# Attention of a two-layer decoder step: rotated rows gathered over two heads' tiles, the sink as a column of the scores, and the stage's instructions in a written order

## The chip, the cores and the metric

The kernel runs on one core of a Trainium2 chip. Its time is device microseconds of one launch; the table below gives the median of three runs and the one profiled execution. All inputs and outputs are float32 in device memory.

## The reference

One inference step of a decoder with two layers, for a prompt of 512 tokens and for 8 samples of one token each (position 2048, with a cached window of 127 + 1 keys). Width 1024, 16 heads of 64, 4 key/value heads, window 128, feed-forward width 2816. Layer 1 mixes tokens by pooling, layer 2 by attention; each layer is feed-forward, mixer, feed-forward. What the change touches is layer 2's attention:

```python
q = _rope((h @ w_q[j]).reshape(B, T, N_KV_HEADS, GROUP, HEAD_DIM), pos)   # rotates dims 0..15 of each 64
s = einsum('bnqkgd,bnskd->bnkgqs', q, k) * (HEAD_DIM ** -0.5)
s = where(mask, s, -inf)                    # d = qpos - kpos: 0 <= d < 128
m = maximum(max(s, -1), sink)               # one sink for each head
p = exp(s - m)
denom = sum(p, -1) + exp(sink - m)
o = einsum('bnkgqs,bnskd->bnqkgd', p / denom, v)
x = x + o @ w_o[j]
```

`_rope` replaces dims 0..7 by x1 cos - x2 sin and dims 8..15 by x2 cos + x1 sin and leaves dims 16..63.

## The kernel before

**Layout.** Activations stand transposed: eight tiles `x[k]` of 128 features by 520 tokens (512 of the prompt, 8 samples). A float32 matrix product is made of three matmuls on a high and a low part of each operand (`terms`, `mm`, L417); `split` (L241) makes the parts, the high one by ScalarE (L245), the low one by VectorE (L246).

**Weights.** The class `Weights` loads chunks of 1 MB on SyncE's queue into three `raw` buffers and splits them piece by piece on ScalarE (`wh`, L194) and VectorE (`wl`, L195), five pieces ahead of their use; `prefetch` is called where a piece is taken. A load is pinned behind what was written before it on SyncE; it waits for its buffer at the head of that queue.

**The order.** The instructions are given in the order of the program to a planner, which may move them by their due times, except those wrapped in `later`: such an instruction is pinned behind the one written just before it on its engine. In the attention stage of before, few are.

**The attention stage** (L1033 to L1341). Eight q tiles of 128 features, t = 0..7, each two heads e = 0, 1 of 64 rows. `q_part(t, h)` makes half of the product (24 matmuls), `q_evac(t)` copies it out of PSUM (L919), rotates it (L920 to L923: multiply by cos, shuffle the rows by 8 within groups of 32, multiply by sin, add, all on 128 rows), splits it, and copies the samples' columns to `qz` (L1063). A `Unit(t, h)` is two blocks of 128 queries of both heads of a tile; there are 16. `scores` (L1086 to L1088) makes 12 matmuls on 64 rows each and 256 keys, of which block 0 needs only 128. `softmax` adds the mask and takes the maximum (L1101, four times), brings it and the sinks together (L1115 to L1117), takes the exponentials with their sums (L1121) and that of the sink (L1129), adds and inverts (L1130, L1131) and scales the four parts (L1134 on ScalarE, L1136 on VectorE). `turn` transposes the scaled parts (L1146) and splits them (`xh`, `xl`). `values` multiplies by v (L1169) and copies to `oT` (L1181). The loop over n = 0..18 calls scores(n), q parts, turn(n-2), jobs, softmax(n), values(n-3) and the evacuations; jobs are the samples' own attention (L1219 to L1265) and the first half of the output product (`o_part(m, 0)`, L1278), of which the second half, `o_part(m, 4)`, follows the loop. PSUM has four pairs of banks (`duo`).

Of the kernel before, what the change touches and what calls it, by code (L numbers as in the profile page):

```python
# [45 lines left out]
C_END = C_AB + 2  # L46
# [7 lines left out]
def shape_constants():  # L54
# [11 lines left out]
    for h in (0, 64):  # L66
        c[h : h + 8, C_COS : C_COS + TOK] = cos
        c[h + 8 : h + 16, C_COS : C_COS + TOK] = cos
        c[h : h + 8, C_SIN : C_SIN + TOK] = -sin
        c[h + 8 : h + 16, C_SIN : C_SIN + TOK] = sin  # L70
    for gi, w in enumerate(WINS):
        for b in range(NS):
            for r in range(15 - (w - 1), 15):
                c[b * 15 + r, C_SEL + gi * NS + b] = 1.0
# [138 lines left out]
def yoco_step(ctx, tc, ins, outs):  # L213
# [26 lines left out]

    def split(dst, src, scale=None):  # L241

        hi, lo = dst
        if scale is None:
            S.activation(hi, src, AF.Copy)  # L245
            V.tensor_tensor(lo, src, hi.bitcast(F32), op=ALU.subtract)  # L246
        else:
            S.activation(hi, src, AF.Copy, scale=scale)
            V.scalar_tensor_tensor(lo, src, scale, hi.bitcast(F32), op0=ALU.mult, op1=ALU.subtract)

    def later(ins):

        return tc.keep_in_program_order(ins)
# [121 lines left out]
    def rstd_tok(t0=0, t1=5):  # L375
# [3 lines left out]
        for t in range(t0, t1):  # L379
            lo = t * P if t < 4 else 400  # L380
            T.matmul(pss[:, t : t + 1], acc[:, lo : lo + P], ones[:, 0:1], start=True, stop=True)  # L381
        v, y, t_ = (cp.tile([P, 5], F32, tag=n, name=n)[:, t0:t1] for n in ("nv", "ny", "nt"))
        later(V.tensor_scalar(v, pss[:, t0:t1], 1.0 / D, EPS, op0=ALU.mult, op1=ALU.add))
        V.tensor_scalar(y.bitcast(I32), v.bitcast(I32), 1, None, op0=ALU.arith_shift_right)
        V.tensor_scalar(y.bitcast(I32), y.bitcast(I32), -1.0, float(0x5F3759DF), op0=ALU.mult, op1=ALU.add)
        for it in range(3):
            V.tensor_tensor(t_, y, y, op=ALU.mult)
            V.scalar_tensor_tensor(t_, t_, -0.5, v, op0=ALU.mult, op1=ALU.mult)
            o = r_tok[:, t0:t1] if it == 2 else y
            V.scalar_tensor_tensor(o, t_, 1.5, y, op0=ALU.add, op1=ALU.mult)  # L390

    def rstd_samples():

        pr2 = pss_[0][:, 0, 8 : 8 + NS]
        T.matmul(pr2, r_tok[:, 4:5].broadcast_to([P, P]), ident[:, 112:120], start=True, stop=True)
        S.copy(R[:, SP:], pr2)
# [16 lines left out]
    def mm(w, kk, mov, banks, first, last, halves=(0, 1), pin=lambda ins: ins):  # L413
# [494 lines left out]
    kT = [kvp.tile([P, TOK], F32, tag="kT", name=f"kT{g}", bufs=2) for g in range(2)]  # L908
# [124 lines left out]
    with tc.tile_pool(name="at", bufs=2) as at:  # L1033
        cst = at.tile([P, 512], F32, name="cst", bufs=1)
        nc.scalar.dma_start(cst, consts[:, C_MASK : C_MASK + 512])
        csq = rawp.tile([P, 2, TOK], F32, tag="raw", name="csq")
        nc.scalar.dma_start(csq.rearrange("p a t -> p (a t)"), consts[:, C_COS : C_COS + 2 * TOK])
# [6 lines left out]

        r8 = at.tile([P, NB], F32, name="r8", bufs=1)
        nr8 = at.tile([P, NB, 2], F32, name="nr8", bufs=1)
        oS = at.tile([P, KT, NS], F32, name="oS", bufs=1)
        oT = [big.tile([P, SP], F32, tag="th", name="oT") for t in range(KT)]
# [6 lines left out]

        def q_evac(t, banks):
            qT = at.tile([P, TOK], F32, tag="qT", name="qT", bufs=1)
            rope(qT, banks, cosq, sinq, at, ("rp0", "rp1"))
            qq = pair(XX, [P, SP])
            split(qq, qT[:, :SP])  # L1060
            for e in range(2):
                rows = slice(e * 64, e * 64 + 64)
                V.tensor_copy(qz[t // 4][rows, e, t % 4, :], qT[rows, SP:])  # L1063
            return qq

        class Unit:
# [6 lines left out]
            def scores(self):  # L1073
# [5 lines left out]
                for bi, b in enumerate(self.bs):  # L1079
                    for e in range(2):  # L1080
                        rows = slice(e * 64, e * 64 + 64)
                        o = self.pe[e][:, bi * 256 : (bi + 1) * 256]
                        qc = slice(b * P, (b + 1) * P)
                        k0 = max(b - 1, 0) * P
                        kc_ = slice(k0, k0 + 256)
                        T.matmul(o, qh[rows, qc], kh[rows, kc_], start=True, stop=False)  # L1086
                        T.matmul(o, ql[rows, qc], kh[rows, kc_], start=False, stop=False)
                        T.matmul(o, qh[rows, qc], kl[rows, kc_], start=False, stop=True)  # L1088

            def softmax(self):  # L1090
                c0 = self.t * 8 + self.h * 4
                mx, nm, es, den = (at.tile([P, 4], F32, tag=n, name=n) for n in ("mx", "nm", "es", "den"))
                self.sms = []
                for bi, b in enumerate(self.bs):
                    if (2 * self.t + self.h) % 3 < 2:
                        sm = at.tile([P, 512], F32, tag="sm", name="sm", bufs=4)
                    else:
                        sm = kvp.tile([P, TOK], F32, tag="kT", name="sm", bufs=2)
                    mk = C_MASK if b == 0 else C_MASK + 256
                    for e in range(2):  # L1100
                        ins = V.tensor_tensor_reduce(  # L1101
                            out=sm[:, e * 256 : (e + 1) * 256],
                            in0=self.pe[e][:, bi * 256 : (bi + 1) * 256],
                            in1=cst[:, mk : mk + 256],
                            op0=ALU.add,
                            op1=ALU.max,
                            scale=1.0,
                            scalar=NEG,
                            accum_out=mx[:, bi * 2 + e : bi * 2 + e + 1],
                        )  # L1110
                        if self.t == 0:
                            later(ins)
                    self.sms.append(sm)
                nr = nr8[:, self.bs[0] : self.bs[1] + 1, :].rearrange("p b e -> p (b e)")
                later(V.tensor_tensor(nm, mx, nr, op=ALU.mult))  # L1115
                later(V.tensor_tensor(nm, nm, nsinks[:, c0 : c0 + 4], op=ALU.min))
                V.tensor_tensor(es, sinks[:, c0 : c0 + 4], nm, op=ALU.add)  # L1117
                part = lambda i: self.sms[i // 2][:, (i % 2) * 256 : (i % 2) * 256 + 256]
                for i in range(4):
                    b = self.bs[i // 2]  # L1120
                    S.activation(  # L1121
                        part(i),
                        part(i),
                        AF.Exp,
                        scale=r8[:, b : b + 1],
                        bias=nm[:, i : i + 1],
                        accum_out=den[:, i : i + 1],
                    )
                S.activation(es, es, AF.Exp)  # L1129
                V.tensor_tensor(den, den, es, op=ALU.add)  # L1130
                V.reciprocal(den, den)  # L1131
                for i in range(4):
                    if i % 2:
                        S.activation(part(i), part(i), AF.Copy, scale=den[:, i : i + 1])  # L1134
                    else:
                        V.tensor_scalar(part(i), part(i), den[:, i : i + 1], None, op0=ALU.mult)  # L1136

            def turn(self):
                self.pts = []
                both = duo()  # L1140
                for bi, b in enumerate(self.bs):
                    kts = (0,) if b == 0 else (0, 1)
                    pt = both[:, bi, :]
                    for kt in kts:
                        for e in range(2):
                            T.transpose(  # L1146
                                pt[:, kt * 256 + e * P : kt * 256 + (e + 1) * P],
# [305 lines left out]
```

## Time and profile before

| | us |
|---|---|
| median of 3 runs | 1697.96 |
| lowest, highest | 1693.47, 1698.41 |
| the profiled execution | 1691.85 |
| its span, first to last instruction | 1690.0 |
| TensorE busy | 1657.5 |
| VectorE busy | 1254.4 |
| ScalarE busy | 903.5 |

The profile's rows name an instruction by the line of the kernel, the engine, the operation and its tiles as out<-in, with partitions x elements. PE is TensorE's matmuls, PEld its weight loads, DVE VectorE, ACT ScalarE, POOL GpSimd, SP SyncE; a q behind an engine's name is its queue. Busy time is the union of the instructions' times; the duration of one includes a start that overlaps the end of the one before. The granted clock is TensorE's, 1.00 being full speed. In the waits stand the total, the number and the longest, in us. Of transfers the rows give KB each and the median time from issue to landing.

### The profile page before, as it was taken

What the parts mean: (1) busy time and instruction counts of PE and PEld (TensorE: products, weight loads), DVE (VectorE), ACT (ScalarE), POOL (GpSimd) and SP (SyncE); (2) the same over time, 40 slices, a digit from 0 to 9 for tenths busy, and PEclk for the clock granted to TensorE, in tenths of its full rate; (3) what the DMA queues carried; (4) which work ended last, traced back from release to release, by engine and by line L of the source; (5) the groups of instructions that cost most, each with busy time, mean ns of one, the idle gap of its engine ahead of it and who ended that gap; (6) DMA issues with size and microseconds to landing.
All of it is one profiled execution on the core that took longest, in us unless ns stands there. A gap on an engine that the chain in (4) does not pass through costs nothing.

```text
span 1690.0 us, 34449 instructions
## 1 busy us (share of the span) xinstructions
PE 1657.5 (98%) x13754; PEld 1642.7 (97%) x13754; DVE 1254.4 (74%) x2452; ACT 903.5 (53%) x1793; POOL 142.3 (8%) x176
## 2 busy tenths in 40 slices
PE   9999999999999999999999999999989999999997
PEld 8999999999999999999999999998879999999996
DVE  6866866887875875888775875888876885785776
ACT  6743643665652652656552652655886653463454
POOL 0101101000101101100101101100000100110100
PEclk9999999999999999999999999999899999999998
DMA  8546745652545855634745845642122554674631
GB/s 214 137 128 142 181 134 136 174 167 80 129 140 129 178 147 130 153 117 129 162 137 125 187 137 127 152 138 71 50 51 76 131 137 131 148 173 132 148 109 52
DMA packets 313327, 224.71 MB, mean 133 GB/s; under 512 B 9152, under 2 KB 289320, under 8 KB 313126
## 3 DMA queue, kind: packets, MB, share of 16 engines
q1 hardware_dynamic: 286416, 176.13, 36.8%
q0 software_dynamic: 22432, 40.26, 14.5%
q10 hardware_dynamic: 4318, 6.12, 1.2%
q8 instruction: 108, 1.77, 0.4%
q14 instruction: 53, 0.43, 0.1%
HBM read 180.11 MB, written 5.04 MB: 110 GB/s over the span
## 4 chain that ended last, share of the span: by engine, by line
PE 90%; DVE 4%; ACT 3%; DMA 1%; issue 1%; DVEq 0%; ACTq 0%
PE ps L443 45%; PE ps L417 41%; ACT sm L1121 1%; PE ps L1169 1%; PE ps L814 1%; DVE wl L195 1%; DMA pr<-in_bands_dram 1%; PE ps L839 1%; DVE sm L1101 1%; DVE xl L246 0%; ACT wh L194 0%; PE ps L1146 0%; PE ps L381 0%; PE ps L698 0%; DMA pr<-in_pool_w_dram 0%
## 5 line engine op out<-in xcount | busy, mean ns | idle before, releaser
L194 ACT ACTIVATE wh<-raw 128x512 fp32r<-128x512 f32 (+1 forms) x736 | 446.3, 621 | 544.8 <-PE ps L417 329.5
L195 DVE TENSOR_TENSOR wl<-raw,wh 128x512 fp32r<-128x512 f32 (+1 forms) x736 | 486.9, 676 | 200.7 <-ACT wh L194 197.2
L443 PE MATMUL ps<-th,wh 128*128 128x260 f32 x1216 | 343.7, 283 | 0.0
L443 PE MATMUL ps<-tl,wh 128*128 128x260 f32 x1216 | 343.1, 282 | 0.0
L443 PE MATMUL ps<-th,wl 128*128 128x260 f32 x1216 | 341.5, 282 | 0.0
L417 PE MATMUL ps<-hh,wh 128*128 128x260 f32 x1376 | 284.3, 285 | 2.3 <-DVE mx L1101 1.0
L417 PE MATMUL ps<-hl,wh 128*128 128x260 f32 x1376 | 283.2, 283 | 0.0
L417 PE MATMUL ps<-hh,wl 128*128 128x260 f32 x1376 | 280.7, 282 | 0.0
L443 PEld LDWEIGHTS ps<-tl,wh 128*128 128x128 f32 x1216 | 229.0, 188 | 0.0
L443 PEld LDWEIGHTS ps<-th,wh 128*128 128x128 f32 x1216 | 228.7, 188 | 0.2 <-ACT sa L523 0.2
L443 PEld LDWEIGHTS ps<-th,wl 128*128 128x128 f32 x1216 | 228.1, 188 | 0.0
L417 PEld LDWEIGHTS ps<-hh,wh 128*128 128x128 f32 x1376 | 213.5, 189 | 4.0 <-DVE mx L1101 1.2
L417 PEld LDWEIGHTS ps<-hl,wh 128*128 128x128 f32 x1376 | 215.2, 189 | 0.1
L417 PEld LDWEIGHTS ps<-hh,wl 128*128 128x128 f32 x1376 | 214.0, 189 | 0.0
L443 PE MATMUL ps<-xh,wh 128*128 128x260 f32 x672 | 188.3, 283 | 0.0
L443 PE MATMUL ps<-xl,wh 128*128 128x260 f32 x672 | 188.2, 283 | 0.0
L443 PE MATMUL ps<-xh,wl 128*128 128x260 f32 x672 | 184.2, 282 | 0.0
L159 POOL DMA_DIRECT2D raw<-raw x76 | 65.5, 862 | 1302.8 <-DMA raw<-in_ffn_w_up_dram 438.9
L417 PE MATMUL ps<-xh,wh 128*128 128x260 f32 x736 | 149.4, 285 | 0.6 <-ACT wh L194 0.6
L417 PE MATMUL ps<-xl,wh 128*128 128x260 f32 x736 | 149.5, 284 | 0.5 <-DVE xl L717 0.5
L417 PE MATMUL ps<-xh,wl 128*128 128x260 f32 x736 | 147.8, 283 | 0.1
L591 DVE TENSOR_TENSOR u<-ps,R 128x520 f32<-128x520 f32 (+1 forms) x99 | 67.2, 681 | 106.3 <-PE ps L417 106.3
(260 smaller groups left out, 2849.1 us busy)
## 6 DMA issues: line engine op xcount, KB each, us to landing
raw<-in_ffn_w_gate_dram SPq DMA_DIRECT2D x87, 512.0 KB, 3.9
raw<-in_ffn_w_up_dram SPq DMA_DIRECT2D x87, 512.0 KB, 5.4
raw<-in_ffn_w_down_dram SPq DMA_DIRECT2D x32, 1024.0 KB, 5.3
raw<-raw POOLq DMA_DIRECT2D x76, 256.0 KB, 3.3
S<-in_ffn_w_up_dram SPq DMA_DIRECT2D x76, 256.0 KB, 5.6
S<-raw POOLq DMA_DIRECT2D x76, 256.0 KB, 4.7
raw<-in_ffn_w_down_dram SPq DMA_DIRECT2D x16, 768.0 KB, 4.9
raw<-in_w_q_dram SPq DMA_DIRECT2D x8, 512.0 KB, 4.0
```

Of the source, the lines that this page charges most:

```text
L159: G.dma_start(blk(raw, 2, 1), blk(raw, 1, 1), accum_op=ALU.add)
L194: self.pin(nc.scalar.activation(dh, src, AF.Copy))
L195: self.pin(nc.vector.tensor_tensor(dl, src, dh.bitcast(F32), op=ALU.subtract))
L417: ins = T.matmul(banks[:, hf, :H], a[:, kk, :], hcols(b, hf), start=(first and i == 0), stop=(last and i == 2),)
L443: T.matmul(bank[:, :H], a[:, kk, :], b, start=(not more and kk == 0 and i == 0), stop=(kk == 3 and i == 2), skip_group_check=more,)
L591: V.tensor_tensor(parts(u), bank[:, hfs[0] : hfs[-1] + 1, :H], parts(R[:, c]), op=ALU.mult)
L814: T.matmul(o, a[:, s], b[:, kk, :], start=(n == 0), stop=(n == 5))
L839: T.matmul(po[:, half * 256 : half * 256 + 256], z[:, tau, c], b, start=(i == 0), stop=(i == len(lst) - 1),)
L1101: ins = V.tensor_tensor_reduce(out=sm[:, e * 256 : (e + 1) * 256], in0=self.pe[e][:, bi * 256 : (bi + 1) * 256], in1=cst[:, mk : mk + 256] ...
L1121: S.activation(part(i), part(i), AF.Exp, scale=r8[:, b : b + 1], bias=nm[:, i : i + 1], accum_out=den[:, i : i + 1],)
L1169: T.matmul(po[:, bi * 256 : (bi + 1) * 256], a, p_[:, kc_], start=(n == 0), stop=(n == 3 * len(kts) - 1),)
```

## The change

- **Rotation.** `q_evac` copies the whole q tile to `qraw` and gathers the rows that rotate: for each of its two heads a strip of 16 rows goes by a transfer on SyncE's queue to a tile of 64 rows that two q tiles share. `q_turn(s)` shuffles, multiplies, multiplies and adds once for the pair of tiles, on 64 rows, and writes the pair's four strips back, two by SyncE's queue and two by GpSimd's. `q_split(t)` then makes the high and low parts and copies the samples' columns on GpSimd. The cos and sin table has 64 rows and stands in a buffer of the stage and not in a `raw` buffer.
- **Sink.** The scores' tile has a 257th column that holds the negated sink. The mask's reduction multiplies by -rstd/8 (a column operand), starts from the negated sink and takes the minimum, so that it yields the bias itself; the exponentials' sums contain the sink's.
- **Scaling** is a step of its own, `scale`, one unit later, all four parts on VectorE. Block 0 uses 128 columns in scores, reduction, exponentials and scaling.
- **Order.** `seq` pins every TensorE, VectorE and ScalarE instruction of the stage up to the loop's end (`ordered`), weight splits included (`W.pin = later`). Seven q parts stand ahead of the first scores, softmax(n) behind scores(n), the samples' and output jobs come later, and the score matmuls alternate between the two heads.

```diff
+    def seq(ins):
+        return later(ins) if ordered[0] else ins
...
-    def mm(w, kk, mov, banks, first, last, halves=(0, 1), pin=lambda ins: ins):
+    def mm(w, kk, mov, banks, first, last, halves=(0, 1), pin=seq):
...
-        csq = rawp.tile([P, 2, TOK], F32, tag="raw", name="csq")
-        nc.scalar.dma_start(csq.rearrange("p a t -> p (a t)"), consts[:, C_COS : C_COS + 2 * TOK])
+        csq = at.tile([64, 2, TOK], F32, name="csq", bufs=1)
+        nc.scalar.dma_start(csq.rearrange("p a t -> p (a t)"), consts[:64, C_CG : C_CG + 2 * TOK])
...
         def q_evac(t, banks):
-            qT = at.tile([P, TOK], F32, tag="qT", name="qT", bufs=1)
-            rope(qT, banks, cosq, sinq, at, ("rp0", "rp1"))
-            qq = pair(XX, [P, SP])
-            split(qq, qT[:, :SP])
+            qraw[t] = big.tile([P, TOK], F32, tag="th", name="qraw")
+            later(S.copy(halves(qraw[t]), banks[:, :, :H]))
+            if t % 2 == 0:
+                turned[t // 2] = at.tile([64, TOK], F32, tag="qT", name="qG", bufs=1)
+            for e, rows in enumerate(strips(qraw[t])):
+                o = t % 2 * 32 + e * 16
+                nc.sync.dma_start(turned[t // 2][o : o + 16, :], rows)
+
+        def q_turn(s):
+            G = turned[s]
+            sw = at.tile([64, TOK], F32, tag="rp0", name="rp1", bufs=1)
+            seq(V.stream_shuffle(sw, G, swap16))
+            seq(V.tensor_tensor(G, G, cosq[:64], op=ALU.mult))
+            seq(V.tensor_tensor(sw, sw, sinq[:64], op=ALU.mult))
+            seq(V.tensor_tensor(G, G, sw, op=ALU.add))
+            for t in (2 * s, 2 * s + 1):
+                for e, rows in enumerate(strips(qraw[t])):
+                    o = t % 2 * 32 + e * 16
+                    if e:
+                        nc.gpsimd.dma_start(rows, G[o : o + 16, :])
+                    else:
+                        nc.sync.dma_start(rows, G[o : o + 16, :])
+
+        def q_split(t):
+            qq[t] = pair(XX, [P, SP])
+            split(qq[t], qraw[t][:, :SP])
             for e in range(2):
                 rows = slice(e * 64, e * 64 + 64)
-                V.tensor_copy(qz[t // 4][rows, e, t % 4, :], qT[rows, SP:])
+                nc.gpsimd.tensor_copy(qz[t // 4][rows, e, t % 4, :], qraw[t][rows, SP:])
...
             def softmax(self):
+                seq(V.tensor_copy(sm[:, :, 256], nsinks[:, c0 : c0 + 4]))
...
+                            op0=ALU.add,
+                            op1=ALU.min,
+                            scale=nr8[:, b : b + 1],
+                            scalar=nsinks[:, c0 + i : c0 + i + 1],
+                            accum_out=nm[:, i : i + 1],
...
-                later(V.tensor_tensor(nm, mx, nr, op=ALU.mult))
-                later(V.tensor_tensor(nm, nm, nsinks[:, c0 : c0 + 4], op=ALU.min))
-                V.tensor_tensor(es, sinks[:, c0 : c0 + 4], nm, op=ALU.add)
...
-                S.activation(es, es, AF.Exp)
-                V.tensor_tensor(den, den, es, op=ALU.add)
...
+            def scale(self):
+                den = self.den
+                seq(V.reciprocal(den, den))
                 for i in range(4):
-                    if i % 2:
-                        S.activation(part(i), part(i), AF.Copy, scale=den[:, i : i + 1])
-                    else:
-                        V.tensor_scalar(part(i), part(i), den[:, i : i + 1], None, op0=ALU.mult)
+                    p_ = self.sms[i][:, : 256 if self.bs[i // 2] else P]
+                    seq(V.tensor_scalar(p_, p_, den[:, i : i + 1], None, op0=ALU.mult))
...
+        ordered[0], W.pin = True, later
         later(S.activation(warm, ones[:, 0:1], AF.Exp))
         for h in (0, 1):
             q_part(0, h)
-        qq[0] = q_evac(0, qb[0])
+        q_evac(0, qb[0])
         rstd_tok()
         q_part(1, 0)
...
         q_part(1, 1)
+        q_evac(1, qb[1])
         rstd_samples()
...
         q_part(2, 0)
+        q_part(2, 1)
+        q_turn(0)
+        q_evac(2, qb[2])
+        q_part(3, 0)
+        q_split(0)
+        q_split(1)
+        q_parts = {n: (3 + (n + 1) // 2, (n + 1) % 2) for n in range(9)}
+        q_evacs = {0: 3, 2: 4, 4: 5, 6: 6, 8: 7}
+        q_turns = {1: 1, 5: 2, 9: 3}
+        q_splits = {2: (2,), 3: (3,), 6: (4,), 7: (5,), 10: (6, 7)}
...
+            11: [lambda: sample_scores(1, 0), lambda: sample_scores(1, 4)],
+            12: [lambda: pr_s.append(sample_softmax()), lambda: o_part(0, 0, (0,))],
+            13: [lambda: sample_turn(pr_s[0]), lambda: o_part(1, 0, (0,))],
+            14: [lambda: sample_values(0), lambda: sample_values(4)],
+            15: [lambda: o_part(0, 0, (1,)), lambda: o_part(1, 0, (1,))],
+            16: [lambda: o_part(2, 0), lambda: o_part(3, 0)],
+            17: [lambda: o_part(4, 0), lambda: o_part(5, 0)],
+            18: [lambda: o_part(6, 0), lambda: o_part(7, 0)],
+        o_splits = {9: (0,), 10: (1,), 11: (2, 3), 13: (4,), 15: (5,), 17: (6,), 18: (7,)}
...
             if n < 2 * KT:
                 units[n].scores()
+                units[n].softmax()
+            if 1 <= n <= 2 * KT:
+                units[n - 1].scale()
+            if n in q_parts:
+                q_part(*q_parts[n])
             if LAG <= n < 2 * KT + LAG:
                 units[n - LAG].turn()
...
+            if VLAG <= n < 18:
                 units[n - VLAG].values()
             if n in q_evacs:
-                qq[q_evacs[n]] = q_evac(q_evacs[n], qb[q_evacs[n]])
+                q_evac(q_evacs[n], qb[q_evacs[n]])
+            if n in q_turns:
+                q_turn(q_turns[n])
+            for t in q_splits.get(n, ()):
+                q_split(t)
...
+        ordered[0], W.pin = False, lambda ins: ins
```

235 lines of the change are left out of this document (110 added, 125 removed).

## Prediction

> **What bounds the kernel now.** I read the page first, then the windows of the stretch that the change touches, then PE's timeline in its worst place, then the waits, the groups and the transfers.
>
> ```profile
> span 1690.0 us, 34449 instructions
> PE 1657.5 (98%) x13754; PEld 1642.7 (97%) x13754; DVE 1254.4 (74%) x2452; ACT 903.5 (53%) x1793; POOL 142.3 (8%) x176
> PE 90%; DVE 4%; ACT 3%; DMA 1%; issue 1%; DVEq 0%; ACTq 0%
> ```
>
> TensorE sets the time nearly everywhere; the chain that ended last runs only 7% of its length on VectorE and ScalarE. The windows say where. The attention stage runs from the first q matmul, at about 1143.0 us, to the last output matmul at about 1317.1.
>
> ```profile
> 1143.00:1159.60 16.60, 16.60 (x142) 16.54 (x139) 10.95 (x25) 8.11 (x14) 0.23 (x2) 1.00 0.24 68
> 1159.60:1270.00 110.40, 97.62 (x786) 87.92 (x785) 89.88 (x357) 85.43 (x246) 0.52 (x1) 0.94 0.21 49
> 1270.00:1317.10 47.10, 47.10 (x398) 47.10 (x397) 34.29 (x71) 31.56 (x71) 0.00 (x0) 1.00 0.32 87
> 1185.00:1190.00 5.00, 2.97 (x13) 2.45 (x13) 3.03 (x11) 4.34 (x13) 0.00 (x0) 0.50 0.52 103
> 1400.00:1500.00 100.00, 100.00 (x838) 100.00 (x837) 67.82 (x113) 42.65 (x79) 12.18 (x14) 1.00 0.66 157
> ```
>
> The columns are length, then busy time (and instructions) of PE, weight loads, DVE, ACT and POOL, then granted clock. Head and tail of the stage are solid matmul. In the 110.4 us between, PE stands open for 12.8 us and its clock falls to 0.94, while DVE is busy 81% and ACT 77% of the time. How much PE time is lost there I count from prices: a saturated stretch issues 838 wide matmuls in 100 us, 0.1193 us each, and the rest of the prices are here:
>
> ```profile
> 1163.09 0.39 PE L1086 MATMUL ps<-tl,xh 64*128 64x256 f32 x2
> ...
> 1164.13 0.51 PE L417 MATMUL ps<-hh,wh 128*128 128x260 f32 x2
> ...
> 1181.99 0.48 PE L1169 MATMUL ps<-xh,tl 128*128 128x256 f32 x2 [2.48 <-ACT xh L245]
> ...
> 1187.38 0.80 PE L1169 MATMUL ps<-xh,tl 128*128 128x256 f32 x2 [2.03 <-ACT xh L245]
> ...
> 1282.51 0.60 PE L1146 MATMUL ps<-ident,sm 128*128 128x128 f32 x4
> 1282.86 0.49 PE L417 MATMUL ps<-hh,wh 128*128 128x260 f32 x2
> ```
>
> A unit's twelve score matmuls take 1164.13 - 1163.09 = 1.04 us (they already run in pairs, one for each half of the rows). Four transposes take 0.35, with the slower start behind them about 0.11 each. The stage has 16 x 48 = 768 projection matmuls and 168 of the values: 936 x 0.1193 = 111.7; scores 16 x 1.04 = 16.6; 112 transposes 12.3; 67 small ones of the samples and 10 of the norm, taken like transposes, 8.5. Sum 149.1 of 174.1 us: **25 us are lost, all in the middle stretch**. The two idle times of 2.48 and 2.03 us above are examples: PE waits for the ACT half of a unit's split, and the granted clock is then 0.50 (the window at 1185), so an idle time is paid about twice. Who is late:
>
> ```profile
> DVE den L1130 <- ACT es L1129: 7.2, 7, 2.2
> ACT xh L245 <- DVE qT L923: 4.8, 2, 2.5
> ACT sm L1121 <- DVE nm L1116: 4.7, 5, 1.6
> PE ps L1169 <- ACT xh L245: 4.5, 2, 2.5
> ```
>
> DVE and ACT wait for each other in turns, in an order that the planner chose, and PE for their sum. So less work on the two, and an order in which each has something ready, is worth PE time here, up to 25 us and nothing outside this stretch.
>
> **The change part by part.** Work on the two engines first (busy time of a whole group, then mean ns of one):
>
> ```profile
> L1101 DVE CUSTOM_DVE_ANT_0 sm<-ps,cst 128x256 f32<-128x256 f32 x64 | 24.0, 419 | 7.9 <-PE ps L1146 4.1 <-PE ps L1088 3.6
> L1136 DVE TENSOR_SCALAR sm<-sm,den 128x256 f32<-128x256 f32 x32 | 9.8, 348 | 0.2
> L921 DVE STREAM_SHUFFLE rp<-rp 128x520 f32<-128x520 f32 x8 | 5.9, 740 | 0.0
> L923 DVE TENSOR_TENSOR qT<-qT,rp 128x520 f32<-128x520 f32 x8 | 5.6, 698 | 0.0
> L922 DVE TENSOR_TENSOR rp<-rp,csq 128x520 f32<-128x520 f32 x8 | 5.6, 694 | 0.0
> L920 DVE TENSOR_TENSOR qT<-rp,csq 128x520 f32<-128x520 f32 x8 | 5.5, 691 | 3.0 <-DMA csq<-in_consts_dram 3.0
> L1063 DVE COPY qz<-qT 64x8 f32<-64x8 f32 x16 | 2.6, 166 | 0.3
> L1130 DVE TENSOR_TENSOR den<-den,es 128x4 f32<-128x4 f32 x16 | 2.6, 160 | 7.5 <-ACT es L1129 7.4
> L1116 DVE TENSOR_TENSOR nm<-nm,nsinks 128x4 f32<-128x4 f32 x16 | 2.4, 157 | 0.2
> L1115 DVE TENSOR_TENSOR nm<-mx,nr 128x4 f32<-128x4 f32 x16 | 2.4, 157 | 0.3 <-ACT sm L1121 0.2
> L1117 DVE TENSOR_TENSOR es<-sinks,nm 128x4 f32<-128x4 f32 x16 | 2.4, 156 | 0.1
> L1134 ACT ACTIVATE sm<-sm,den 128x256 f32<-128x256 f32 x32 | 14.4, 500 | 2.2 <-DVE nm L1116 1.1 <-DVE den L1131 1.0
> L1129 ACT ACTIVATE es<-es 128x4 f32<-128x4 f32 x16 | 3.0, 190 | 0.0
> L919 ACT COPY rp<-ps 128x520 f32<-128x520 f32 x8 | 4.6, 573 | 0.0
> L195 DVE TENSOR_TENSOR wl<-raw,wh 128x512 fp32r<-128x512 f32 x32 | 21.8, 686 | 3.2 <-ACT wh L194 3.1
> ```
>
> Rotation: four DVE operations for each of 8 q tiles (5.9 + 5.6 + 5.6 + 5.5 = 22.6) become four for each of 4 pairs, on 64 rows; the columns set the cost, so -11.3. The qz copies go to POOL, -2.6. Sink as a column: L1115, L1116, L1117 and L1130 go, -9.8; one copy of four sinks for each unit comes, at most 16 x 0.17 = +2.7. The reduction takes its scale and start from columns instead of constants; the trace has no such form; between 0 more and the 0.08 by which a four-column operation lengthens, 64 x 0.08 = 5; I take 0, since L1136 with a column operand is no dearer than its width says. All 64 scalings now go to DVE: +9.8. The first block's 16 reductions and 16 scalings are half as wide: by the slope between 419 ns for 256 columns and 157 for four, 0.13 each, -4.2. DVE net: -15.4. ACT loses L1134 (14.4) and L1129 (3.0) and about 16 x 0.11 of exponentials: -19.2. Groups overlap at their ends (DVE's groups of the stage sum to about 159 us for 135 busy), so the engines gain 0.85 of that: DVE 89.9 - 13 = 77, ACT 85.4 - 16 = 69 in a stretch where PE needs 110.4 - 25 = 85. PE itself saves 24 score pairs at half width, about 1.3: 84. **PE becomes the engine with most work in the stretch**, DVE is at 0.91 of it. That is the gain's condition, and what is left to lose is order.
>
> The written order, walked through. *Start.* Seven q parts (24 matmuls, 2.86 each) and the norm (1.0) now stand ahead of the first scores: PE reaches them at 1143.0 + 20.0 + 1.0 = 1164. What they need is a chain with two transfers, which the trace of before does not hold; their ends are these:
>
> ```profile
> kc<-knew POOLq DMA_DIRECT2D x4, 2.0 KB, 1.8
> raw<-in_w_o_dram SPq DMA_DIRECT2D x8, 512.0 KB, 5.3
> ```
>
> A strip is 16 rows of 2 KB, 33 KB; nearer the small one, I take 2.5. Tile 1's q is done at 1155.5, its copy at 1156.1, the gather at 1158.6. But the DVE queue has a weight split ahead of the turn (wl, 0.69), whose ACT half must wait for the PE part before it, at 1158.4: the turn runs from 1159.7 to 1162.3, the write-back lands at 1164.8 and the first split is done at 1166. So PE stalls 2 us (0 with 1.8 a hop, 6 with 5.3), and a stall of that size halved the clock at 1182: 2 more. While DVE waits for the gather, the weight splits queue behind it and nobody misses them: five pieces, 14 us of PE work, are split ahead.
>
> By the Trainium skill, page "TensorE: Matmul & The Clock Gate", section "Part 1: The HAM clock gate", the clock only falls after an idle window of about 3.4 us; by it the second 2 us of the start would not be paid and the gain would be 16.3 instead of 14.3. The trace disagrees: the clock was 0.50 after an idle time of 2.48.
>
> *Steps 0 to 8* (scores n, softmax n, scaling n-1, a q part, turn n-2, values n-3): PE has 1.04 + 2.86 + 7 x 0.11 + 10.5 x 0.119 = 5.9 us a step. DVE has reductions and sinks 4 x 0.375 + 0.17 - 0.13 = 1.54, scalings and reciprocal 4 x 0.31 + 0.16 - 0.13 = 1.27, the turn's splits 1.24 (two like L195, one of them half as wide in every other unit), a weight split 0.69 and a quarter of a pair's turn and two splits, 1.05: 5.8, by the 0.85 of overlap 4.9. ACT, at 69 for PE's 84, is about as busy. Each consumer comes a step behind its producer, so a wait of some 5 us is hidden. The next pairs' two hops and turn (2.5 + 2.5 + 2.5) have two steps. I charge 2 us for all nine. *Steps 9 to 15*: no q parts; PE has 7 x 1.04 for scores, 50 transposes 5.5, 72 matmuls of values 8.6, two output halves twice 5.7 and the samples 3.3, 30.4 in all. DVE has 7 x (1.54 + 1.27 + 1.24), the last turn 2.8, two q splits and six output splits 5.5, two additions to x and two weight splits 2.8 and about 2 for the samples, 41.5, by 0.85 35.3. Two of the four PSUM pairs are held by halves of the output product from step 12 to 15. I charge the difference of 4.9 and 1.1 for the samples' chain, 6. *Steps 16 to 18* and the rest are output matmuls as solid as the tail of before: 0.
>
> Sum: 25 + 1.3 - (2 + 2 + 2 + 6) = **14.3 us less**: the profiled execution's 1691.85 (span 1690.0) becomes about 1677.5. The median of the runs shown is 6.1 above the profiled one, so I state 1697.96 - 14.3, rounded: **1684**. Without any loss of order it would be 26 less: 1672.
>
> Queues moved past: SP gets 24 small transfers among its weight loads, POOL 8 write-backs and the 16 qz copies. POOL's copies are wanted only by the sample scores from step 8. The rotation table leaves the raw buffers, which frees one of three for weights and ends the 3.0 us that L920 waited; PE was in q parts then, so this is worth nothing. If a write-back on POOL comes 0.35 late twice, it costs 0.7 at the start only. The Trainium skill, page "SBUF — State Buffer", section "SBUF: two separate sides", says that a transfer issued from GpSimd waits while VectorE copies in a two-port mode; by it the gain would be 13.6. The 1.8 us of kc<-knew, also issued from POOL, gives no sign of it.
>
> **The rivals.** *No change*: the fixed order waits as often as the planner's did, because with DVE at 0.91 of PE any hop that comes late is in the way of everything queued behind it. If half of the 16 steps lost 1.6 us more (the longest wait of an exponential for nm above), 13 us, the gain is 1: 1697. For it: the waits above are of the kind ACT for DVE for ACT, which an order cannot remove. Against: turn and values now come one full step after what they need. *Slower*: the strips get stuck in a queue. These are SP's own waits now, and POOL's:
>
> ```profile
> SPq L259 <- DVE wl L195: 69.8, 4, 24.6
> SPq L1296 <- DVE wl L195: 30.9, 1, 30.9
> POOL vc L1297 <- DMA vc<-in_cache_v_win_dram: 71.7, 1, 71.7
> ```
>
> A weight load waits up to 24.6 us at the head of SP for its buffer, harmless today, since only loads are behind it. If a strip is put behind such a load, its pair's scores come late by 24.6 less the step of 5.9 that hides it, and 2 for the clock: 20.7 lost against the 14.3 gained, 1704. It decides from a wait of 18 us on. POOL's row is the same danger: a small transfer that waits 71.7 us for a load, with later pairs' write-backs in its queue. Against it: the strips are not pinned behind the loads, and if the planner places a transfer when its data are ready, strips come first; the waits are long only because nothing else calls for the queue. *That the change does less than it says* would need the gathered table to be wrong; nothing in the diff points there.
>
> **How the numbers follow.** Forecast 0.72, no change 0.13, slower 0.15. 0.3% (5 us) is about what a measurement tells from no change: faster than 1692.9 has the forecast's 0.72 and a little of the second case, 0.74; within, 0.11; slower than 1703, 0.15. The range goes from no loss of order, 1672, to 1703, where the second case ends; about 0.18 is outside, mostly above.
>
> **What would show it.** Right: the middle stretch shorter by about 14 us with PE over 93% busy, DVE's busy time down by about 13 and ACT's by 16, L1134, L1129 and the four small sink operations gone, the clock at 1.00 save near the first scores, a PE wait of 2 to 4 us there for a split, and DVE nearly solid in steps 9 to 11. Wrong: SP waiting on a weight load with strips behind it, PE waits for splits of q in the middle, a low clock in several windows, or DVE's reduction much over 419 ns.

## The result, and the profile after

| | before | after |
|---|---|---|
| median, us | 1697.06 (1693.47 to 1698.41) | 1756.07 (1752.04 to 1756.51) |
| profiled: span, us | 1690.0 | 1754.6 |
| mean granted clock in the span | 0.992 | 0.972 |

After to before is 1.0355, 95% interval 1.0337 to 1.0374: the changed kernel is 59 us slower. Line numbers are those of each kernel: the transposes of `turn`, L1146 before, are L1181 after. The page of after, the same lines as were shown of before:

```profile
span 1754.6 us, 34435 instructions
PE 1682.6 (96%) x13754; PEld 1667.0 (95%) x13754; DVE 1255.0 (72%) x2399; ACT 885.8 (50%) x1745; POOL 149.5 (9%) x200
PE 90%; DVE 5%; ACT 3%; DMA 1%; issue 1%; ACTq 0%; DVEq 0%; POOLq 0%
```

TensorE executes the same 13754 matmuls and is busy 25 us longer, so they run slower, and it stands open for 72 us instead of 32. The windows of after (the attention stage, then its head, its middle from just before the first idle time to the last values, and its tail) show where:

```profile
1145.00:1382.70 237.70, 184.26 (x1321) 173.95 (x1320) 136.14 (x397) 107.77 (x281) 7.89 (x27) 0.83 0.19 48
1145.00:1165.60 20.60, 20.60 (x176) 20.60 (x175) 10.41 (x29) 8.96 (x16) 0.23 (x2) 1.00 0.44 104
1165.60:1354.00 188.40, 134.96 (x908) 124.65 (x907) 103.84 (x333) 80.55 (x234) 7.65 (x25) 0.78 0.14 34
1354.00:1382.70 28.70, 28.70 (x242) 28.70 (x241) 21.89 (x36) 18.25 (x32) 0.00 (x0) 1.00 0.36 98
```

The stage takes 237.7 us for 174.1 before. Head and tail are solid at full clock; in the middle no engine is full (PE 72%, DVE 55%, ACT 43%) and the clock is 0.78. The engines wait for each other. PE's waits, the two longest rows of the whole program:

```profile
PE ps L1181 <- DVE xl L263: 49.7, 16, 5.9
PE ps L1128 <- ACT xh L262: 3.3, 1, 3.3
```

The second row is the start that the prediction charged 2 us. The first is new: 16 waits, one for each unit. L1181 is the transposes of `turn`. One of them in after's timeline (start, duration, engine, line, then in brackets the idle time and its releaser):

```profile
1193.70 0.60 PE L1181 MATMUL ps<-ident,sm 128*128 128x128 f32 x4
...
1194.35 0.59 ACT L262 ACTIVATE xh<-ps 128x512 fp32r<-128x512 f32 x1
1194.47 0.69 DVE L202 TENSOR_TENSOR wl<-raw,wh 128x512 fp32r<-128x512 f32 x1 [0.20 <-ACT wh L201]
1195.08 0.68 DVE L263 TENSOR_TENSOR xl<-ps,xh 128x512 fp32r<-128x512 f32 x1
...
1195.82 0.66 PE L1181 MATMUL ps<-ident,sm 128*128 128x128 f32 x4 [1.52 <-DVE xl L263]
...
1203.70 0.66 PE L1181 MATMUL ps<-ident,sm 128*128 128x128 f32 x4 [1.99 <-DVE xl L263]
```

The first block's four transposes (two, in the eight units that hold block 0) are followed by its split, high part on ScalarE, low part on VectorE behind a weight split, and only then do the second block's four transposes start. Both groups write halves of one PSUM tile, `both`, and the split reads its first half. The matmuls behind stand in the written order and can't pass. The last row is the next unit's second group. In the kernel before the same groups stand apart too, but PE has other work between them:

```profile
1200.76 0.60 PE L1146 MATMUL ps<-ident,sm 128*128 128x128 f32 x4
1201.55 0.50 PE L1169 MATMUL ps<-xh,tl 128*128 128x256 f32 x2 [0.20 <-DVE mx L1101]
...
1203.73 0.51 PE L417 MATMUL ps<-hh,wh 128*128 128x260 f32 x2
...
1206.73 0.82 PE L1146 MATMUL ps<-ident,sm 128*128 128x128 f32 x6
```

Values, scores and a projection part fill the 6 us from the first block's four transposes to the second block's, which are four of the six at 1206.73. The planner had put them there; the written order puts the two groups side by side.

### The profile page after: what moved, and what is told of

The parts are those of the page before. It is cut to its first block, busy times and chain, and to the rows that moved or that the text cites. A ratio compares the mean times of both kernels' runs of the same rounds, so it can differ in the third digit from the quotient of the medians.

```text
span 1754.6 us, 34435 instructions
## 1 busy us (share of the span) xinstructions
PE 1682.6 (96%) x13754; PEld 1667.0 (95%) x13754; DVE 1255.0 (72%) x2399; ACT 885.8 (50%) x1745; POOL 149.5 (9%) x200
## 3 DMA queue, kind: packets, MB, share of 16 engines
q10 hardware_dynamic: 4254, 5.86, 1.1%
## 4 chain that ended last, share of the span: by engine, by line
PE 90%; DVE 5%; ACT 3%; DMA 1%; issue 1%; ACTq 0%; DVEq 0%; POOLq 0%
PE ps L456 43%; PE ps L430 40%; PE ps L1206 2%; PE ps L1181 1%; ACT sm L1160 1%; DVE sm L1146 1%; DVE xl L263 1%; PE ps L827 1%; DMA pr<-in_bands_dram 1%; PE ps L852 1%; DVE wl L202 1%; DVE sm L1170 0%; ACT xh L262 0%; PE ps L1302 0%; PE ps L1128 0%
## 5 line engine op out<-in xcount | busy, mean ns | idle before, releaser
L456 PE MATMUL ps<-xh,wl 128*128 128x260 f32 x672 | 184.1, 282 | 0.0
```

What stands on the lines that cost most here:

```text
L456: T.matmul(bank[:, :H], a[:, kk, :], b, start=(not more and kk == 0 and i == 0), stop=(kk == 3 and i == 2), skip_group_check=more,)
```

## Experiments

Each kernel ran beside the kernel before on the same chip (medians 1692.96 to 1694.62); the ratio is to those runs. In the traces the stage starts anywhere from 1142 to 1149 us, whatever is in it, so where one trace stands for a kernel its stage is compared by its own length, from the first q matmul to the last of the output. All the rest of the program takes 1514 to 1521 us in these traces, which is a scatter that every time below holds and the length of a stage does not. The changed kernel itself ran only beside the 1697.06 above, so a difference of its median to one of the medians below carries some 3 us of that.

**Transposes together.** In `turn` of after, all transposes stand ahead of both splits:

```diff
-    n = len(kts) * 256
-    split(tuple(z[:, :n] for z in pp), pt[:, :n])      # inside the loop over the two blocks
+for bi, b in enumerate(self.bs):                       # after it
+    n = 256 if b == 0 else 512
+    split(tuple(z[:, :n] for z in pp), both[:, bi, :n])
```

> The changed kernel with one edit: a turn issues the transposes of both its blocks before the first split. Theory A (the second block's transposes wait for the first block's split, since both write one PSUM tile, and the written order leaves nothing between): the 49.7 us of PE waits for the low half of a split go, the clock comes back to about 1.00, and the time falls from 1756 to 1672-1700. Theory B (the splits are late because VectorE's and ScalarE's queues are behind; the tile is beside the point): the waits move to the values and the time stays over 1735.

Measured 1713.15 (1711.12 to 1716.6), ratio 1.0118 (1.0092 to 1.0144): by the medians 43 us are gone, by the stage too (194.8 us for 237.7), and so is the row of 49.7. It stays 20 us above the kernel before, and so above the range of theory A, though far below B.

**Values between.** In place of that, the values of the unit before are put between the two blocks' transposes:

```diff
-units[n - LAG].turn()
+units[n - LAG].turn(0)
+units[n - VLAG].values()
+units[n - LAG].turn(1)
```

> The changed kernel with the values of unit n-3 put between the two blocks' transposes of unit n-2; the dependency stays. Theory A: 1.05 to 1.4 us of values cover most of a wait of 1.5 us at full clock, so at most 0.5 us a unit is left: 1680-1710. Theory B: over 1735.

Measured 1720.2, ratio 1.0156 (1.0136 to 1.0176). The row falls by more than half:

```profile
PE ps L1183 <- DVE xl L263: 20.9, 14, 3.6
```

A unit's values, nine or twelve matmuls, cover the rest of it. The same mechanism, less of the gain; the result lies above theory A's range, since a wait of 1.5 us is left where 0.5 was reckoned.

**The planner's order.** After without the pinning:

```diff
-ordered[0], W.pin = True, later
```

> The changed kernel without the written order (nothing of the stage pinned but the copies of q): rotation over gathered rows, sink column and scaling on VectorE alone, in the planner's order. Theory A: the planner puts other matmuls between the blocks as it did before, so the time is near the kernel before, with the 15 us less of engine work perhaps seen: 1680-1703. Theory B (engines or the gather's transfers are what is late): over 1720.

Measured 1708.0, ratio 1.0083 (1.0056 to 1.0111). The written order as it stood cost 48 us against the planner's (45 by the stage, 192.6 us here). Another 15 us over the kernel before remain without any pinning, outside both ranges: they come from what the instructions do or from the sequence in which the planner is given them.

**Transposes together in the kernel before:**

> The kernel before with the turn's transposes ahead of its splits. Theory A: the planner already filled these waits, of the 25 us lost only a part hangs on them: 1685-1703. Theory B: 1697, no change.

Measured 1692.18, ratio 0.999 (0.9978 to 1.0003). Where the planner covers the wait, it costs nothing.

**A PSUM tile for each block.** After with its order untouched:

```diff
-both = duo()
-    pt = both[:, bi, :]
+    pt = ps()
```

> The changed kernel (1756.07), its order untouched, with a PSUM tile of its own for the transposes of each of the two blocks, instead of the two halves of one. Theory T (the second group waited for the first block's split only because the halves are one tile): the row of 49.7 us in the waits goes, and the time comes to 1705 to 1722, near the 1713 of the kernel with the transposes together; a unit then takes one PSUM tile more of the four, so some waits for a free tile come in their place. Rival R (the second group waits for the split whichever tile it writes, because of the order of the work on the engines, or for want of a free tile): 1740 to 1765.

Measured 1708.49, ratio 1.0087 (1.0067 to 1.0107). Waits and stage of this kernel:

```profile
PE ps L1180 <- DVE nm L1146: 4.2, 2, 2.6
PE ps L1128 <- ACT xh L262: 3.4, 1, 3.4
PE ps L1128 <- DVE nm L1146: 3.2, 2, 2.5
PE ps L1180 <- DVE xl L263: 0.4, 1, 0.4
```

```profile
1143.30:1334.30 191.00, 167.80 (x1322) 159.90 (x1320) 134.18 (x397) 105.56 (x282) 7.92 (x27) 0.91 0.24 59
```

Of the 16 waits of transposes for `xl` one of 0.4 us is left, with the order of the engines as it was. The shared tile was the cause: it ties the second half to the reader of the first. With it gone the clock of the stage is 0.91 instead of 0.83 and the written order is as good as the planner's.

**Which part holds the other 15 us.** Two counterparts in the planner's order: before with the new scores and softmax alone (its scaling directly behind), and after with the old ones, so that it has the gathered rotation and the new sequence.

> The kernel before, in its planner's order, with its own rotation and sequence of steps, and of the change only the new scores, softmax and scaling (sink as a column, block 0 at half width, all scalings on VectorE). It tells which part holds the 15 us that the change still costs in the planner's order (1708.0 against 1692.96). Theory S (the rotation by gather and the sequence built around it: scores start 10 us later, at 1170.1 instead of 1159.7, and three projection quarters are used up as its cover): without the gather the new softmax is worth its saved work or nothing, 1675 to 1693. Theory X (the new softmax itself: the reduction takes 541 ns instead of 419 ns, so 64 of them cost 7.8 us on VectorE, and the two scalings that ScalarE made now stand behind them in the chain from scores to transposes): 1700 to 1712.

> The counterpart: the changed kernel in the planner's order with the gathered rotation and the new sequence of steps, but scores, softmax and scaling as before. Theory S: the cost stays, 1703 to 1715. Theory X: it goes, 1680 to 1695. Both parts at fault: this kernel and the softmax-only one each at 1697 to 1703.

Measured 1697.81, ratio 1.001 (0.9997 to 1.0024), and 1708.73, ratio 1.0093 (1.0068 to 1.0119). The first interval holds 1: no gain or loss of the new softmax alone can be told, and the time lies between the ranges of S and X. The loss is in the rotation and its sequence. Then the sequence without the gather (the cos and sin table goes back to a `raw` buffer with it):

```diff
-later(S.copy(halves(qraw[t]), banks[:, :, :H]))      # and the strips, q_turn and its write-backs
+rope(qraw[t], banks, cosq, sinq, at, ("rp0", "rp1"))
```

> The gather-and-sequence kernel (1708.73) with the gather taken out: each projection tile is rotated by itself on VectorE as before, at the place where its rows were copied out, and the split stays at its later place; softmax as before, planner's order. It parts the gather from the sequence of steps built around it. Theory G (the two hops of strips and the shared rotation of a pair delay the first scores and the later splits; without them the planner starts the scores early again): 1690 to 1698. Theory Q (the sequence: three quarters of a projection ahead of the first scores, samples and output parts a step later, so that less TensorE work is left between the steps): 1702 to 1712. VectorE does about 15 us more work here than with the gather (8 rotations of four 0.69 us passes instead of 4), so a result at or below 1698 can't come from less work.

Measured 1697.09, ratio 1.0021 (1.0011 to 1.0032), in theory G's range. The stages of the gather-and-sequence kernel and of this one, in this order:

```profile
1143.20:1333.50 190.30, 169.52 (x1321) 157.79 (x1320) 125.68 (x415) 126.89 (x329) 8.37 (x27) 0.92 0.25 61
```

```profile
1148.80:1328.00 179.20, 168.21 (x1321) 158.52 (x1320) 135.12 (x435) 125.78 (x330) 4.21 (x19) 0.92 0.24 60
```

With the gather VectorE is busy 9.4 us less and the stage is 11.1 us longer. The sequence alone leaves 5 us over the 174.1 of before. The largest wait that comes with the gather, in that kernel's timeline:

```profile
1167.34 1.14 SPq L1083 DMA_DIRECT2D qG<-qraw  x2
1168.57 1.35 SPq L272 DMA_DIRECT2D raw<-in_w_o_dram  x2
1169.97 2.20 SPq L1083 DMA_DIRECT2D qG<-qraw  x2
...
1176.96 0.01 DVE L1088 LOAD_MASK_SELECT rp<-qG  x1 [3.49 <-DMA qG<-qraw]
1176.99 0.72 DVE L1088 STREAM_SHUFFLE rp<-qG 64x520 f32<-64x520 f32 x1
1177.61 0.14 DVE L1156 TENSOR_TENSOR nm<-mx,nr 128x4 f32<-128x4 f32 x1
...
1177.86 0.60 ACT L1162 ACTIVATE sm<-sm,nm,r 128x256 f32<-128x256 f32 x1 [4.32 <-DVE nm L1157]
...
1182.58 0.48 PE L1187 MATMUL ps<-ident,sm 128*128 128x128 f32 x1 [5.51 <-DVE sm L1177]
```

A weight load is issued between the strips of tiles 2 and 3. The second pair of strips, issued by 1172.2, arrives at 1176.96, 4.8 us later. VectorE stands 3.49 us at the head of its queue for it, with the softmax of a unit queued behind: `nm` comes at 1177.61, ScalarE starts the exponentials after 4.32 us of idling, and PE stands 5.51 us in front of the transposes. VectorE's waits for strips in this kernel, and in the planned version of the whole change:

```profile
DVE rp L1088 <- DMA qG<-qraw: 8.7, 3, 3.7
DVE rp L1088 <- DMA qG<-qraw: 11.0, 3, 4.4
```

Last, the same kernel with tiles 0 and 1 rotated directly:

> The gather-and-sequence kernel (1708.73) with tiles 0 and 1 rotated directly on VectorE, each by itself, and the other three pairs gathered. The kernel with all tiles direct took 1697.09. Theory start (the gather costs where nothing covers it, ahead of the first scores: 5.5 us of idle TensorE in front of the first transposes and a clock of 0.83 behind it): 1697 to 1702. Rival (every pair's gather costs 2.5 to 3 us, by the later splits): 1704 to 1708.

Measured 1703.4, ratio 1.0053 (1.0033 to 1.0073), between both theories: the first pair takes 0.4% (7 us) and the other three 0.3% (5 us); by the stage, 185.6 us here, 5 and 6. Neither theory alone holds. VectorE's wait for strips is nearly gone in this kernel:

```profile
DVE rp L1099 <- DMA qG<-qraw: 1.8, 1, 1.8
```

So that wait goes with the first pair's part of the loss, and can be only a small part of what the other three pairs cost. PE waits 5.7 us for the values' copies on ScalarE in this trace and 1.9 in the one without the gather, but no run tells whether the gather does that.

**What is left of the written order, once mended.** Values ahead of the turn, then also one more projection quarter ahead of the first scores:

> The written order with the transposes of a turn together (1713.15), and in each step the values of the unit before are issued ahead of the turn, so that their two copies on ScalarE stand ahead of the turn's splits. In the trace of the kernel without this edit TensorE waits 8.9 us for the copies of the values (5.1, 2.4 and 1.4 us in three rows), which stand behind two splits of 0.6 us and their partners on VectorE. Theory O (what is left in the written order is the place of these copies in ScalarE's queue): 1696 to 1706. Rival (the copies only came last by a little, and VectorE's chain or the start is what is left): 1710 to 1718.

> The kernel with the values first, and a further projection quarter, about 5.6 us of matmuls, moved from step 0 to ahead of the first scores, so that the start's wait for the gathered rows (3.3 us, and a clock of 0.83 in 1160 to 1180) is covered. Theory start (the uncovered start costs its stall and as much again by the clock): 6 us less than the kernel with the values first. Rival (the quarter is then missing between the first steps, and the stall comes back there): within 2 us of it, or slower.

Measured 1706.16, ratio 1.0078 (1.0051 to 1.0105), and 1704.36, ratio 1.0062 (1.004 to 1.0083). The copies behind the splits were worth 7 us, by the stage too (187.8 us for 194.8), at the end of the range given. Covering the start gained 2 us, as the rival said, which the intervals do not tell from nothing, and the stage is as long as it was (187.7). Rotating the first pair directly there:

> The written order with transposes together and values first (1706.16), tiles 0 and 1 rotated directly and split at once, so that the first scores wait for no strips; the other three pairs are gathered. In the kernel without this edit the first scores wait 3.2 us for the split. Theory start: 1698 to 1702. Rival (a wait in the steps takes its place, as with the quarter moved ahead, which gained 2 us): 1703 to 1707.

Measured 1704.81, ratio 1.0061 (1.0041 to 1.0081): by the medians next to nothing again, as the rival said. In the trace the start's wait is gone and the stage is 184.1 us, 3.7 shorter, in an execution whose rest took 5 us more. So the start accounts for 3 to 4 us at most, and 10 us over the 174.1 of before are elsewhere. In the written order with own tiles PE's waits in the stage sum to 12 us for reductions (`nm`) and 11 for splits, the start's 3.4 among them; before they are 3 (`mx`) and 6. VectorE waits for strips 2.0 us, once. What lengthens the way to the reductions no run has parted.

**Sharing the scalings again.** Two of four on ScalarE, in the softmax-only kernel (planner's order) and in the best written one:

```diff
-seq(V.tensor_scalar(p_, p_, den[:, i : i + 1], None, op0=ALU.mult))
+if i % 2:
+    seq(S.activation(p_, p_, AF.Copy, scale=den[:, i : i + 1]))
+else:
+    seq(V.tensor_scalar(p_, p_, den[:, i : i + 1], None, op0=ALU.mult))
```

> The softmax-only kernel (1697.81) with two of the four scalings of a unit back on ScalarE, as in the kernel before. Theory B (VectorE's load between 1180 and 1240, 97% in that kernel's trace at 1200 to 1240, is what eats the saved work; two scalings of 0.349 us in 16 units are 10 us of it): 1684 to 1693. Theory N (VectorE's load does not decide, the length of the chain does, and it is as long on ScalarE): 1695 to 1700.

> The best written order so far (1704.36: transposes together, values first, one more quarter ahead of the first scores) with two of the four scalings back on ScalarE. In its trace VectorE is busy 73 to 83% of the steps and TensorE waits 10 us for reductions (2.9, 2.8 and 2.1 us in three rows and less in others). Theory B (VectorE's load delays the reductions): 1695 to 1701. Theory N: 1702 to 1708, and above if ScalarE's fixed queue now holds the splits behind the scalings.

Measured 1691.12, ratio 0.9982 (0.9972 to 0.9993), and 1715.33, ratio 1.0123 (1.0109 to 1.0138). By the ratios the same edit gains 5 us in the planner's order and loses 10 in the written one. There the scalings take their fixed place in ScalarE's queue, and PE's waits for the values' copies on ScalarE come back (8.0 us for 3.5). The stages of the planned kernels, all scalings on VectorE and shared:

```profile
1147.70:1323.20 175.50, 163.37 (x1321) 155.62 (x1320) 141.96 (x432) 105.36 (x281) 0.76 (x3) 0.93 0.24 61
```

```profile
1143.10:1315.40 172.30, 160.58 (x1321) 152.16 (x1320) 134.31 (x400) 117.02 (x314) 0.75 (x3) 0.96 0.25 62
```

VectorE loses 7.7 us of busy time and the stage 3.2.

**Smaller parts.** Block 0 at half width alone in the kernel before; the shared version with its sample copies on GpSimd; and with the sink copies there too:

> The kernel before with one part of the change alone: block 0 at half width (scores, reduction, exponential and scalings over 128 columns instead of 256 in 8 of 16 units). It saves 16 halves of a reduction, an exponential and a scaling, some 2 us on VectorE, 3 on ScalarE and 3 on TensorE, and adds nothing. If TensorE's own time counts: 1688 to 1692 against 1693. If the waits hide it: 1692 to 1695.

> The kernel with the new softmax and shared scalings, planner's order, no gather (1691.12), with the 16 copies of the rotated sample columns (64x8) on GpSimd instead of VectorE, as the change has them. They take some 0.1 us each on VectorE, 2 us in all. If VectorE's load still counts: 1688 to 1691. If not: 1691 to 1694.

> The best version so far (new softmax with shared scalings, sample copies on GpSimd, no gather: 1690.34) with the 16 copies of the sink column (128x4, 0.163 us each on VectorE, 2.4 us in all) on GpSimd too. If VectorE's load counts: 1688 to 1690. If not, 1690 to 1692; above that if the exponential comes to wait for GpSimd.

Measured 1694.15, ratio 1.0007 (0.9995 to 1.0018): nothing. 1690.34, ratio 0.9979 (0.9967 to 0.999): no step beyond the version without it can be told. 1691.35, ratio 0.9991 (0.9979 to 1.0003): nothing. The best versions are thus 0.2% ahead of the kernel before, less than the 0.3% that I called measurable, though two intervals lie below 1; their stages are 172.3 to 173.5 us for 174.1.

## Why the prediction was wrong, by its own steps

**What bounds the kernel: right.** TensorE's time in this stage is the stage, waits on the split chains cost it, and the clock charges an idle time again. That its 25 us could be had is not shown: no version took more than 2 us off the stage.

**The step that failed: PE's time in a turn.** The prediction wrote 7 x 0.11 us for the transposes of a step, taken from a row of four in a row, and never asked what the fifth waits for. The trace gave one warning, unread: the groups of before are x4 with other work behind them. Both groups share a tile, so in a fixed order a step holds a chain of transposes, ScalarE's half, VectorE's half, four transposes. It came 16 times at 3.1 us, 49.7 in all, where 0 stood. Own tiles or transposes together took 43 to 48 us off.

**The second failed step: the gather's cover.** The size of a hop, 2.5 us, was near the traces (strips landed in a median of 1.8 to 2.0; the first row is of the gather kernel, the others of after):

```profile
qG<-qraw SPq DMA_DIRECT2D x16, 32.5 KB, 2.0
qraw<-qG SPq DMA_DIRECT2D x8, 32.5 KB, 2.0
qraw<-qG POOLq DMA_DIRECT2D x8, 32.5 KB, 1.8
```

The prediction let VectorE wait for it at the start, with only weight splits queued behind that nobody misses, and gave the later pairs two steps of cover. In the planner's order softmax stood behind it: the gather cost 11 us of the stage (12 by the medians), about half of it with the first pair, and VectorE stood 8.7 to 11.0 us for strips. In the changed kernel that wait is small, and it is not what made it slow:

```profile
DVE rp L1088 <- DMA qG<-qraw: 1.9, 1, 1.9
```

So this step failed in the kernels in the planner's order. Why the written order, once mended, still stays 10 to 15 us above the kernel before, where 14 us less were forecast, is open. The slower rival was half right: a pair of strips behind a weight load landed after 4.8 us instead of 2. But no strip was seen stuck at the head of SyncE's queue behind a load that waits for its buffer; it was VectorE that stood.

**Terms of the sum.** The reduction with column operands was taken at 0 more, within 0 to 0.08 us:

```profile
L1146 DVE CUSTOM_DVE_ANT_0 sm<-ps,cst,nsinks 128x256 f32<-128x256 f32 x48 | 23.6, 541 | 9.0 <-PE ps L1128 9.0
L1146 DVE CUSTOM_DVE_ANT_0 sm<-ps,cst,nsinks 128x128 f32<-128x128 f32 x16 | 5.9, 404 | 0.8 <-PE ps L1128 0.8
L1160 ACT ACTIVATE sm<-sm,nm 128x257 f32<-128x257 f32 x48 | 23.9, 500 | 8.7 <-DVE nm L1146 8.7
L1088 DVE STREAM_SHUFFLE rp<-qG 64x520 f32<-64x520 f32 x4 | 3.0, 738 | 0.0
L1137 DVE COPY sm<-nsinks 128x4 f32<-128x4 f32 x16 | 2.6, 163 | 0.0
```

It is 0.12 more than the 419 of before, outside the range: 29.5 us where 21.9 were reckoned, half of the net saving of 15.4 on VectorE. Against it the exponential became cheaper, 500 for the 590 of this row of before (4 us more off ScalarE than reckoned); its scale is now a constant, and it has one column more:

```profile
L1121 ACT ACTIVATE sm<-sm,nm,r 128x256 f32<-128x256 f32 x64 | 37.6, 590 | 4.8 <-DVE nm L1116 4.7
```

The shuffle on 64 rows takes as long as on 128, as assumed, and the sink's copy 0.163. VectorE's busy time in the stage did not fall at all: 136.1 for 135.1 (the three windows shown of before, added). The sum of its durations fell by 5.5, from 163.7 to 158.2 over all records, but operations that stand apart do not overlap at their ends, as the factor 0.85 had assumed.

**The start: nearly right**, 3.3 us for 2 charged, with a lower clock behind it. *Steps 9 to 15* were charged 6 us as VectorE's load; VectorE was half idle there (50.4 us busy of the 100 from 1240 to 1340), so its load did not decide; nine of the 16 waits of the turn end in these 100 us. *The range* had nothing for a dependence inside a helper whose tile and split the change left as they were, and no case of it among the rivals; "no change" came nearest in kind (a wait that an order cannot remove) but priced half of the steps at 1.6 us.

**Signs.** Of what would show it wrong, two came: a low clock in several windows, and the reduction well over 419. PE did wait for splits in the middle, but for those of the turn and not of q, as the sign had it.

## What to carry to other kernels

Before pinning an order that a planner used to choose, list for each instruction what it waits for, tile by tile, also in the helpers that the change leaves alone: a wait that cost nothing under other work is paid in full, once for each unit, when its cover is moved. Count a transfer that an engine consumes not by its own length but by what is queued behind the instruction that waits for it. And saved busy time on engines that stand in a chain is worth little until the chain is shorter: here 9 us less VectorE time came with a stage 11 us longer.

## What the runs showed of the hardware

The clock fell after idle times of 2 us. Four windows of after, around the pair of groups whose second waits 1.99 us at 1203.70:

```profile
1200.00:1202.00 2.00, 1.71 (x15) 1.47 (x13) 1.97 (x11) 1.80 (x9) 0.00 (x0) 1.00 0.80 151
1202.00:1204.00 2.00, 0.30 (x3) 0.30 (x4) 1.64 (x5) 0.97 (x3) 0.00 (x0) 1.00 0.01 4
1204.00:1206.00 2.00, 2.00 (x16) 2.00 (x14) 0.77 (x2) 0.60 (x1) 0.00 (x0) 0.72 0.00 0
1206.00:1208.00 2.00, 2.00 (x15) 1.55 (x14) 0.00 (x0) 1.32 (x3) 0.00 (x0) 0.50 0.00 0
```

PE is nearly empty for one window, and two windows later runs at half speed although it works again; the 1.52 us of the pair at 1195.82 left it at 1.00. The Trainium skill, page "TensorE: Matmul & The Clock Gate", section "Part 1: The HAM clock gate", gives an idle window of about 3.4 us for this; the trace shows the drop after 1.99. Of the 16 waits of the turn those of 1.41, 1.52 and 1.75 us left the clock at 1.00, and all others, 1.99 to 5.86, were followed by 0.50. One length alone is no threshold: in the kernel before, idle times of 0.73 and 1.48 us, 1 us apart, were followed by 0.50 too, from 1238 to 1240. Repeated in most steps, such waits kept the mean at 0.78 for 188 us, which is how 49.7 us of waits came with 25 us more of busy time.

Two operand forms have prices that no trace of before showed: a reduction with a column for its scale and one for its start 0.12 us more than with constants (541 and 419 ns; it also takes the minimum in place of the maximum, which no run parts), an exponential with a constant scale 0.09 us less than with a column (500 and 590 ns).
